# Row norms of the first layer's input from token-major squares on ScalarE, and another order of the first three column chunks

## The chip, the core and the metric

The kernel runs on one core of a Trainium2 chip. The metric is device time in microseconds (us), the median of several executions. The engines are named as the profile names them: PE (TensorE), ACT (ScalarE), DVE (VectorE), POOL (GpSimd) and SP (SyncE, which issues most of the transfers).

## What is computed

A trunk of two layers over 256 tokens of width 2048, in float32. Layer 0 is attention, layer 1 a spatial gating unit. What matters here is the start of layer 0: the RMS norm of the input, one projection, and the norms of the heads.

```python
def _rms(x, g):
    xf = x.astype(jnp.float32)
    y = xf * lax.rsqrt(jnp.mean(xf * xf, axis=-1, keepdims=True) + EPS)
    return y * g.astype(jnp.float32)

def _even_layer(x, ln_g, w_in, qk_g, sinks, w_out, rel_bias):
    h = _rms(x, ln_g).astype(x.dtype)
    z = h @ w_in
    ...
    qa, ka, va, ga, qb, kb, vb, gb = jnp.split(z, cuts, axis=-1)
    ya = _mixer_a(qa, ka, va, qk_g[0], qk_g[1], sinks, rel_bias[:, :A_HEADS])
    yb = _mixer_b(qb, kb, vb, qk_g[2], qk_g[3], rel_bias[:, A_HEADS:])
    y = jnp.concatenate([ya * jax.nn.silu(ga), yb * jax.nn.silu(gb)], axis=-1)
    return x + y.astype(x.dtype) @ w_out
```

The 16 query heads of mixer A fill two column chunks of 512, its two key and value heads together one narrow chunk of 256 columns.

## The kernel before

**Products.** A product is done one column chunk at a time (`gemm`, L100): 512 columns of weights, all 16 k tiles of 128 rows, for the two token tiles of 128. Float32 operands are split into two parts, `hi` and `lo`, and three matmuls stand for one product: `hi` by `whi` (L121), `hi` by `wlo` (L122), `lo` by `whi` (L123). A chunk has 96 matmuls, 12 for each pair of k tiles; a pair is called a tile below, numbered 0 to 7 within a chunk. Its weights come in one transfer on SP's queue (L80) into `wraw` (6 buffers); ACT casts them into `whi` (L85) and DVE subtracts to get `wlo` (L86), 4 buffers each. The two accumulators of a chunk take two of the four PSUM banks `g`; so a chunk cannot start before the chunk before the last has been copied out.

**The first chunk.** In chunk QA, the first 512 query columns of mixer A, `pre0` runs ahead of each tile. `load_hT` (L147) loads a piece of x transposed (`xT`, 256 KB), and ACT and DVE multiply it by the norm's gain and split it (`hTh` L159, `hTl` L160). The row norm itself is left out of `h`: it is applied as a scale when accumulators are copied out by ACT (`evac`, L204), so it is needed only then. `add_squares` (L171) makes it from the same transposed x: POOL squares (L175, L178) and adds up (L179) into `sqa`.

**The second chunk and the norm.** `in0` of QA is followed by the narrow k/v chunk of mixer A (`w_kva`). While it runs, `first_evac` (L113) adds up `sqa` over the partitions by eight small matmuls against `ones` (`sum_squares`, L185), DVE makes the reciprocal root (`row_rstd`, `rsqrt`), and ACT copies QA out. After that chunk come the norms of the k heads and of the q heads (`headnorm`: square on POOL L214, sums L216 and roots on DVE; `scaled`: POOL L224), then the second query chunk, QA1, the gates GA0 and GA1, and mixer B's chunks KB, QB, VB.

**The order around it.** Attention is put between matmuls by `fillers`, generators of which `gemm` advances one step twice per tile. The steps of mixer A's first half begin after the k/v chunk, wait 20 fills (`WAIT0`) and then transpose keys (`k_T`) and queries (`q_T`, L234) on PE through the single bank `t`. x itself, token major (`xr`), is wanted for the residual; its two halves of 1 MB are loaded by `load_x` (L191), written after the gates. The instructions are placed by a scheduler: each engine works in the order that it gives, and the parts of one step are spread between those of others.

Of the kernel before, what the change touches and what calls it, by code (L numbers as in the profile page):

```python
# [10 lines left out]
F32 = mybir.dt.float32  # L11
# [6 lines left out]
P = 128  # L18
S = 256
# [9 lines left out]
MAXD = 2048  # L29
L1, L2, WAIT0, WQ, WAITS = 3, 5, 20, 2, 2  # L30


@with_exitstack
def trunk(ctx, tc, x, xT, ev_g, w_in0, w_kva, qk_g, sinks, w_out0, od_g, w_in1, v_g, w_sT, b_s,
# [13 lines left out]
    def m2(shape, name):  # L48
        return mid.tile(shape, F32, tag="m2", name=name)
# [10 lines left out]
    def rsqrt(xin, n, scale):  # L60
        """(scale * xin + EPS) ** -0.5 for a [128, n] tile."""
        a = tiny.tile([P, n], F32, tag=f"ra{n}", name=nm("ra"))
        nc.vector.tensor_scalar(a, xin, scale, EPS, op0=ALU.mult, op1=ALU.add)
        y = tiny.tile([P, n], F32, tag=f"ry{n}", name=nm("ry"))
        nc.vector.tensor_scalar(y.bitcast(I32), a.bitcast(I32), -0.5, float(0x5F3759DF),
                                op0=ALU.mult, op1=ALU.add)
        t = tiny.tile([P, n], F32, tag=f"rt{n}", name=nm("rt"))
        for _ in range(3):
            nc.vector.tensor_tensor(t, y, y, op=ALU.mult)
            nc.vector.scalar_tensor_tensor(t, t, -0.5, a, op0=ALU.mult, op1=ALU.mult)  # L70
            nc.vector.scalar_tensor_tensor(y, t, 1.5, y, op0=ALU.add, op1=ALU.mult)
        return y

# [1 line left out]
    def wtile(w, kt, cw, fine=False):  # L75
# [24 lines left out]
    def gemm(aT, nkt, w, cw, pre=None, last=False):  # L100
        """act [256, 128 * nkt] @ one column chunk w (cw columns, tiled by _tiles);
        aT(kt) gives the (hi, lo) parts of act^T."""
        # (PSUM bank, token tile, first and last column)
        acc = [(psum("g", 4), 0, 0, cw), (psum("g", 4), 1, 0, cw // 2 if last else cw)]
        if last:
            acc.append((psum("g", 4), 1, cw // 2, cw))
        for k0 in range(0, nkt, 2):
            if pre is not None:
                pre(k0)
            fine = pre is not None and k0 == 0  # L110
            whi, wlo = wtile(w, k0, cw, fine)
            work = [(g, k) for g in acc for k in range(2)]
            if fine:  # L113
                work.sort(key=lambda t: t[1])
            for n, ((bank, tt, a, b), k) in enumerate(work):
                kt = k0 + k
                ah, al = aT(kt)
                sl = slice(tt * P, (tt + 1) * P)
                st, en = kt == 0, kt == nkt - 1
                o = bank[:, :b - a]  # L120
                nc.tensor.matmul(o, ah[:, sl], whi[:, k, a:b], start=st, stop=False)  # L121
                nc.tensor.matmul(o, ah[:, sl], wlo[:, k, a:b], start=False, stop=False)  # L122
                nc.tensor.matmul(o, al[:, sl], whi[:, k, a:b], start=False, stop=en)  # L123
                if n % 2:
                    fill()
        return acc if last else [g[0] for g in acc]

# [1 line left out]
    # The tensor engine's clock and the activation table are warm when the first data arrive.  # L129
    wz = cons.tile([P, P], F32, name="wz")  # L130
# [10 lines left out]

    xr = cons.tile([P, 2, D], F32, name="xr")      # residual stream, token major

# [3 lines left out]
    def load_hT(kt):  # L147
        """Normalisation gain on x^T, split; two k tiles at a time."""
        q, r = divmod(kt, 4)
# [16 lines left out]

    ones = cons.tile([P, 2], F32, name="ones")
    nc.vector.memset(ones, 1.0)
    sqa = cons.tile([P, 2, S], F32, name="sqa")

    def add_squares(kt):  # L171
        """Sum of squares of x^T over k tiles, two at a time."""
        raw = xTt[kt // 4][:, kt % 4:kt % 4 + 2, :]
        if kt == 0:
            nc.gpsimd.tensor_tensor(sqa, raw, raw, op=ALU.mult)  # L175
        else:
            sq = m2([P, 2, S], nm("sqx"))
            nc.gpsimd.tensor_tensor(sq, raw, raw, op=ALU.mult)  # L178
            nc.gpsimd.tensor_tensor(sqa, sqa, sq, op=ALU.add)  # L179

    def sum_squares():
        tp = psum("t", 1)
        for tt in range(2):
            for j in range(2):
                nc.tensor.matmul(tp[:, 2 * tt:2 * tt + 2], sqa[:, j, tt * P:(tt + 1) * P], ones,  # L185
                                 start=j == 0, stop=j == 1)
        ss0 = cons.tile([P, 2, 1], F32, name="ss0")
        nc.vector.tensor_copy(ss0, tp[:, 0:4].rearrange("p (t c) -> p t c", c=2)[:, :, 0:1])
        return ss0

# [3 lines left out]
    def row_rstd(ss, n, name):  # L194
        """ss [128, 2, m]: partial sums of squares over n columns."""
        s2 = cons.tile([P, 2], F32, name=name + "s")
        nc.vector.tensor_reduce(s2, ss, axis=AX.X, op=ALU.add)
        r = rsqrt(s2, 2, 1.0 / n)
        keep = cons.tile([P, 2], F32, name=name)
        nc.vector.tensor_copy(keep, r)  # L200
        return keep

# [1 line left out]
    def evac(acc, cw, func=AF.Copy, name="z", rs=None):  # L204
# [5 lines left out]
    def headnorm(z, nh):  # L210
        """z: [128, 2, nh*64] in place times its per-head rsqrt."""
        sq = c4([P, 2, 512], nm("sq"))
# [25 lines left out]
    def q_T(z, scale, box):  # L238
        """Queries of token tile 0 in float32, of tile 1 in two float32r parts."""
        q0 = c4([P, 4, P], nm("q0"))  # L240
# [43 lines left out]
    def bias_tile(mix, h):  # L284
        """Position bias of four heads, with the mask (and multiplicities) added."""
        bt = c4([P, 4, 256], nm("bias"))
        nc.gpsimd.dma_start(bt, bias[(mix * 16 + h) // 4].rearrange("p (h k) -> p h k", h=4))
        nc.gpsimd.tensor_tensor(bt, bt, ba[:, mix:mix + 1, :].broadcast_to([P, 4, 256]), op=ALU.add)  # L288
        return bt

    def attention(mix, h0, first_bias, qTb, kTb, vfn, ydst):
        """Eight heads h0.. of one mixer; ydst: [128, 2, 512] output (ungated)."""
        (q0, q1), (k0, kh, kl) = qTb, kTb
# [92 lines left out]
    def split_T(y, yT, q, tags):  # L386
        """y [128 tok, 2, 512] -> yT[q] = (hi, lo), each [128, 4, 256]."""
        hi, lo = c4([P, 4, S], nm("yTh"), F32R), c4([P, 4, S], nm("yTl"), F32R)
# [13 lines left out]

    QA, GA, QB, KB, VB, GB = 0, 2, 4, 6, 8, 10     # first column chunk in w_in0

# [9 lines left out]

    def pre0(k0):
        load_hT(k0)
        add_squares(k0)

    acc = in0(QA, pre0)
    box = []  # L420

    def first_evac():
        for _ in range(WAITS):
            yield
        rs = row_rstd(sum_squares(), D, "rstd0")
        box.append(rs)
        box.append(evac(acc, 512, rs=rs, name="qa"))

    fillers.append(first_evac())
    acc1 = gemm(hTk, KT, w_kva, 256)  # L430
    rs, zq = box
    qkg = cons.tile([P, 4], F32, name="qkg")
# [10 lines left out]
    dup = ka_norm(zkv)  # L443
    qk_norm(zq)
    kTa = []
# [41 lines left out]
    fillers.append(attn_a(0, zq))  # L487
    zq1 = qk_norm(evac(in0(QA + 1), 512, rs=rs, name="qa"))
    fillers.append(attn_a(1, zq1))
    gates(0, 0)  # L490
    load_x(0)
    gates(0, 1)
    load_x(1)
    for g in range(2):
# [8 lines left out]

# [1 line left out]
    g1 = cons.tile([P, KT], F32, name="g1")  # L505
# [43 lines left out]

# [1 line left out]
    rs1 = row_rstd(ss1, D, "rstd1")  # L551
# [70 lines left out]

# [1 line left out]
    for q in range(4):  # L624
# [17 lines left out]
def _tiles(w, cw):  # L642
    """[K, N] -> [N / cw, K / 256, 128, 2 * cw]: each two k tiles of a column chunk in one block."""
    k, n = w.shape
# [4 lines left out]
def _layout(x, ev_ln_g, ev_w_in, ev_qk_g, ev_sinks, ev_w_out, od_ln_g, od_w_in, od_v_g, od_w_s,  # L649
# [50 lines left out]
```

## Time and profile before

| what | value |
|---|---|
| median of 3 runs | 1183.59 us (1182.34 to 1183.89) |
| profiled execution, first to last instruction | 1182.0 us span |
| the median over that span | 1.6 us |
| busy in the span: PE, DVE, ACT, POOL | 1166.1, 661.6, 592.3, 158.8 us |
| mean DMA rate | 185 GB/s |

The profile's page gives no other time for the profiled execution than its span. The view of waits lists who waited for whom; the timeline gives each instruction by start and duration, both in us, and in brackets the idle time ahead of it and what ended that. A matmul's duration contains its way through the pipeline: matmuls of 512 columns with about 0.4 us each start about 0.23 us apart, and so the distance of starts is what a matmul costs.

### The profile page before, as it was taken

How to read it: one execution, taken by the hardware profiler on the slowest of the kernel's cores; microseconds unless marked ns; L12 is line 12 of the kernel's file. 1: busy time of each engine (PE TensorE's matmuls, PEld its weight loads, DVE VectorE, ACT ScalarE, POOL GpSimd, SP SyncE). 2: the span in 40 equal slices, each digit the busy share in tenths (PEclk: the TensorE clock that was granted, in tenths of full speed). 3: DMA queues.
4: the chain of work that ended last, by engine and by line, in shares of the span. 5: the costliest groups of instructions: out<-in, count | busy, mean ns of one | idle time of the engine just before them, and what ended most of it. 6: DMA issues, size and time to landing. Idle time of an engine off the chain costs nothing.

```text
span 1182.0 us, 14627 instructions
## 1 busy us (share of the span) xinstructions
PE 1166.1 (99%) x5554; PEld 964.1 (82%) x5554; DVE 661.6 (56%) x839; ACT 592.3 (50%) x804; POOL 158.8 (13%) x100
## 2 busy tenths in 40 slices
PE   7999999999999999999999999999999999999998
PEld 5877788788788888888888888888888888888887
DVE  8685556656645555455455655556555555544443
ACT  5447654464554454554554555454455545433332
POOL 7141201202203000021123211000000000000000
PEclk9999999999999999999999999999999999999999
DMA  7873435625526555666665545555554555566661
GB/s 252 269 255 110 143 127 180 224 91 183 207 94 213 203 180 184 201 203 213 204 199 178 210 171 189 185 188 182 177 193 162 194 194 181 184 211 201 206 212 37
DMA packets 63638, 218.37 MB, mean 185 GB/s; under 512 B 7632, under 2 KB 10320, under 8 KB 63312
## 3 DMA queue, kind: packets, MB, share of 16 engines
q1 hardware_dynamic: 60352, 209.74, 52.1%
q0 software_dynamic: 2080, 7.34, 1.9%
q8 instruction: 43, 0.70, 0.2%
q10 hardware_dynamic: 1136, 0.36, 0.1%
q14 instruction: 27, 0.22, 0.1%
HBM read 215.32 MB, written 2.10 MB: 184 GB/s over the span
## 4 chain that ended last, share of the span: by engine, by line
PE 92%; DVE 3%; DMA 1%; issue 1%; ACT 1%; POOL 1%; SPq 0%; ACTq 0%; DVEq 0%; POOLq 0%
PE g L121 28%; PE g L122 28%; PE g L123 28%; DVE wlo L86 1%; POOL wsn L587 1%; PE t L341 1%; PE s L312 1%; PE u L356 1%; DMA g<-in_od_g_dram 1%; PE u L357 1%; PE t L393 1%; PE s L315 1%; PE u L355 1%; ACT whi L85 1%; PE t L234 0%
## 5 line engine op out<-in xcount | busy, mean ns | idle before, releaser
L86 DVE TENSOR_TENSOR wlo<-wraw,whi 128x1024 fp32r<-128x1024 f32 (+1 forms) x393 | 520.8, 1329 | 425.8 <-ACT whi L85 425.4
L85 ACT CAST whi<-wraw 128x1024 fp32r<-128x1024 f32 (+1 forms) x393 | 408.4, 1041 | 494.1 <-PE g L123 474.5
L122 PE MATMUL g<-wlo,hTh 128*128 128x512 f32 (+1 forms) x1184 | 460.9, 389 | 7.0 <-DVE wlo L86 7.0
L121 PE MATMUL g<-whi,hTh 128*128 128x512 f32 (+1 forms) x1184 | 465.2, 393 | 0.0
L123 PE MATMUL g<-whi,hTl 128*128 128x512 f32 (+1 forms) x1184 | 460.1, 389 | 0.0
L122 PEld LDWEIGHTS g<-wlo,hTh 128*128 128x128 f32 x1184 | 223.0, 188 | 51.2 <-DVE wlo L86 9.6
L121 PEld LDWEIGHTS g<-whi,hTh 128*128 128x128 f32 x1184 | 222.8, 188 | 45.4 <-ACT whi L85 0.6
L123 PEld LDWEIGHTS g<-whi,hTl 128*128 128x128 f32 x1184 | 222.9, 188 | 44.6
L121 PE MATMUL g<-whi,yTh 128*128 128x512 f32 (+1 forms) x416 | 156.1, 375 | 0.0
L122 PE MATMUL g<-wlo,yTh 128*128 128x512 f32 (+1 forms) x416 | 155.3, 373 | 0.0
L123 PE MATMUL g<-whi,yTl 128*128 128x512 f32 (+1 forms) x416 | 155.2, 373 | 0.0
L121 PEld LDWEIGHTS g<-whi,yTh 128*128 128x128 f32 x416 | 78.4, 188 | 13.7
L123 PEld LDWEIGHTS g<-whi,yTl 128*128 128x128 f32 x416 | 78.3, 188 | 13.8
L122 PEld LDWEIGHTS g<-wlo,yTh 128*128 128x128 f32 x416 | 78.4, 188 | 13.6
L611 POOL TENSOR_TENSOR y<-y,gt 128x1024 f32<-128x1024 f32 x8 | 19.2, 2406 | 265.2 <-ACT gt L207 265.2
L575 POOL TENSOR_TENSOR v<-v,gv 128x1024 f32<-128x1024 f32 x8 | 21.9, 2743 | 220.1 <-ACT junk L572 220.1
L318 DVE CUSTOM_DVE_ANT_0 sb<-s,bias 128x256 f32<-128x256 f32 x32 | 13.5, 422 | 28.8 <-PE s L315 28.8
L587 POOL TENSOR_SCALAR wsn<-ws,rstdv 128x256 f32<-128x256 f32 x16 | 20.3, 1280 | 60.7 <-PE s L601 57.3
L331 ACT ACTIVATE pr<-sb,nmx 128x256 f32<-128x256 f32 x32 | 16.3, 508 | 23.0 <-DVE nmx L329 13.7
L207 ACT ACT_TABLE_LOAD x21 | 26.9, 1283 | 1.7 <-PE g L123 1.4
L288 POOL TENSOR_TENSOR bias<-bias,ba 128x1024 f32<-128x1024 f32 x8 | 20.8, 2599 | 37.7 <-DMA bias<-in_bias_dram 37.7
L593 DVE TENSOR_TENSOR vl<-v,vh 128x1024 fp32r<-128x1024 f32 x8 | 9.8, 1226 | 16.4 <-ACT vh L592 16.4
(135 smaller groups left out, 652.6 us busy)
## 6 DMA issues: line engine op xcount, KB each, us to landing
wraw<-in_w_in_dram SPq DMA_DIRECT2D x287, 512.0 KB, 4.0
wraw<-in_w_out_dram SPq DMA_DIRECT2D x96, 512.0 KB, 3.5
bias<-in_bias_dram POOLq DMA_DIRECT2D x8, 512.0 KB, 4.4
xT<-in_xT_dram SPq DMA_DIRECT2D x8, 256.0 KB, 5.1
wraw<-in_w_kva_dram SPq DMA_DIRECT2D x8, 256.0 KB, 4.2
xr<-in_x_dram SPq DMA_DIRECT2D x2, 1024.0 KB, 7.0
gv<-in_v_g_dram POOLq DMA_DIRECT2D x8, 256.0 KB, 3.0
out_dram<-o SPq DMA_DIRECT2D x7, 256.0 KB, 4.9
```

The lines of the kernel that those rows point to most:

```text
L85: nc.scalar.copy(hi[:, js, :cw], raw[:, js, :cw])
L86: nc.vector.tensor_tensor(lo[:, js, :cw], raw[:, js, :cw], hi[:, js, :cw].bitcast(F32), op=ALU.subtract)
L121: nc.tensor.matmul(o, ah[:, sl], whi[:, k, a:b], start=st, stop=False)
L122: nc.tensor.matmul(o, ah[:, sl], wlo[:, k, a:b], start=False, stop=False)
L123: nc.tensor.matmul(o, al[:, sl], whi[:, k, a:b], start=False, stop=en)
L207: nc.scalar.activation(z[:, tt, :cw], acc[tt][:, :cw], func, scale=rs[:, tt:tt + 1])
L288: nc.gpsimd.tensor_tensor(bt, bt, ba[:, mix:mix + 1, :].broadcast_to([P, 4, 256]), op=ALU.add)
L318: nc.vector.tensor_tensor_reduce(out=sb[:, 0:256], in0=sp[:, 0:256], in1=bt[:, j, :], scale=1.0, scalar=NEG, op0=ALU.add, op1=ALU.max, acc ...
L331: nc.scalar.activation(pr[:, 0:256], sb[:, 0:256], AF.Exp, bias=nmx[:, j, 1:2], accum_out=l[:, j, 1:2])
L575: nc.gpsimd.tensor_tensor(v, v, gv.unsqueeze(1).broadcast_to([P, 2, 512]), op=ALU.mult)
L587: nc.gpsimd.tensor_scalar(wsn[:, n], ws[c // 4][:, (2 * c) % 8:(2 * c) % 8 + 2, :], rsv[:, n:n + 1], None, op0=ALU.mult)
L611: nc.gpsimd.tensor_tensor(y, y, gate[0], op=ALU.mult)
```

## The change

The squares of transposed x on POOL and their sum on PE are removed. Instead each half of x in token-major form is loaded during the second chunk, and ACT squares it in four pieces with the sums of each row as a second output (`accum_out`). The second chunk is now QA1 (512 query columns), and the narrow k/v chunk the third. `X0` fills go by before the first half of x is loaded, and `XW` between a load and its Squares; with 16 fills in a chunk, the load and the Squares of the second half are written right behind chunk QA1. The later loads of x are gone, and the norm of the second q chunk follows that of k. The rest of the diff removes comments.

```diff
-L1, L2, WAIT0, WQ, WAITS = 3, 5, 20, 2, 2
+L1, L2, WAIT0, WQ, X0, XW = 3, 5, 20, 2, 4, 8
...
-    ones = cons.tile([P, 2], F32, name="ones")
-    nc.vector.memset(ones, 1.0)
-    sqa = cons.tile([P, 2, S], F32, name="sqa")
...
-            nc.gpsimd.tensor_tensor(sq, raw, raw, op=ALU.mult)
-            nc.gpsimd.tensor_tensor(sqa, sqa, sq, op=ALU.add)
...
-                nc.tensor.matmul(tp[:, 2 * tt:2 * tt + 2], sqa[:, j, tt * P:(tt + 1) * P], ones,
-                                 start=j == 0, stop=j == 1)
...
+    ss0 = cons.tile([P, 2, 4], F32, name="ss0")
+
+    def row_squares(tt, j):
+        junk = m2([P, 512], nm("junk"))
+        nc.scalar.activation(junk, xr[:, tt, j * 512:(j + 1) * 512], AF.Square,
+                             accum_out=ss0[:, tt, j:j + 1])
...
-    acc = in0(QA, pre0)
+    acc = in0(QA, load_hT)
     box = []
 
     def first_evac():
-        for _ in range(WAITS):
-            yield
-        rs = row_rstd(sum_squares(), D, "rstd0")
+        for _ in range(X0):
+            yield
+        for tt in range(2):
+            load_x(tt)
+            for _ in range(XW):
+                yield
+            for j in range(4):
+                row_squares(tt, j)
+                yield
+        rs = row_rstd(ss0, D, "rstd0")
         box.append(rs)
         box.append(evac(acc, 512, rs=rs, name="qa"))
 
     fillers.append(first_evac())
+    accq = in0(QA + 1)
+    while len(box) < 2:
+        fill()
+    rs, zq = box
+    zq1 = evac(accq, 512, rs=rs, name="qa")
+    qk_norm(zq)
     acc1 = gemm(hTk, KT, w_kva, 256)
-    rs, zq = box
...
     dup = ka_norm(zkv)
-    qk_norm(zq)
+    qk_norm(zq1)
...
     fillers.append(attn_a(0, zq))
-    zq1 = qk_norm(evac(in0(QA + 1), 512, rs=rs, name="qa"))
     fillers.append(attn_a(1, zq1))
     gates(0, 0)
-    load_x(0)
     gates(0, 1)
-    load_x(1)
```

How the instructions stand on three engines, of before and of the change (a number behind a name tells instances of a tile apart; line numbers are those of each kernel, the changed one has fewer lines):

POOL from the program's start. Before:

```order
masks.py:199 AFFINE_SELECT ident<-ident 128x128
L175 TENSOR_TENSOR sqa<-xT_104 128x512
L178 TENSOR_TENSOR sqx_137<-xT_104 128x512
L178 TENSOR_TENSOR sqx_166<-xT_160 128x512
L179 TENSOR_TENSOR sqa<-sqa,sqx_137 128x512
L179 TENSOR_TENSOR sqa<-sqa,sqx_166 128x512
L178 TENSOR_TENSOR sqx_192<-xT_160 128x512
L179 TENSOR_TENSOR sqa<-sqa,sqx_192 128x512
```

The change:

```order
masks.py:199 AFFINE_SELECT ident<-ident 128x128
L198 TENSOR_TENSOR sq_487<-qa_481 128x1024
L208 TENSOR_TENSOR qa_481<-qa_481,ry_493 128x1024
L198 TENSOR_TENSOR sq_664<-kva_661 128x2x128
L260 TENSOR_TENSOR kdup_682<-kva_661,ry_670 128x2x128 x2
```

POOL has nothing left in the first chunk; its first work is the head norm of QA, followed by that of k.

ACT from the end of the second chunk's casts to the copies of the chunks. Before (`whi_463` and `whi_481` are the last narrow casts, `whi_553` is the first of QA1, `g_100` and `g_101` hold QA):

```order
L85 CAST whi_463<-wraw_461 128x2x256
L85 CAST whi_481<-wraw_479 128x2x256
L207 ACTIVATE qa_380<-g_100,rstd_378 128x512
L207 ACTIVATE qa_380<-g_101,rstd_378 128x512
L85 CAST whi_553<-wraw_551 128x1024
L85 CAST whi_574<-wraw_572 128x1024
L85 CAST whi_592<-wraw_590 128x1024
L207 ACTIVATE kva_506<-g_323,rstd_378 128x256
L207 ACTIVATE kva_506<-g_324,rstd_378 128x256
```

The change (`whi_434` is QA1's last cast, `whi_510` the first narrow one, `g_98` and `g_99` hold QA, `g_299` and `g_300` QA1):

```order
L85 CAST whi_434<-wraw_432 128x1024
L172 ACTIVATE junk_455,ss_97<-xr 128x512
L172 ACTIVATE junk_457,ss_97<-xr 128x512
L172 ACTIVATE junk_459,ss_97<-xr 128x512
L172 ACTIVATE junk_461,ss_97<-xr 128x512
L85 CAST whi_510<-wraw_508 128x2x256
L85 CAST whi_528<-wraw_526 128x2x256
L191 ACTIVATE qa_481<-g_98,rstd_479 128x512
L191 ACTIVATE qa_481<-g_99,rstd_479 128x512
L85 CAST whi_546<-wraw_544 128x2x256
L191 ACTIVATE qa_484<-g_299,rstd_479 128x512
L191 ACTIVATE qa_484<-g_300,rstd_479 128x512
```

Four Squares stand between QA1's casts and the narrow ones, and both query chunks are copied out among the narrow casts.

DVE around the transposed keys of mixer A (`kl`). Before (`rt_709` and `ry_707` belong to the norm of QA1's heads):

```order
L71 SCALAR_TENSOR_TENSOR ry_707<-rt_709,ry_707 128x16
L69 TENSOR_TENSOR rt_709<-ry_707 128x16
L86 TENSOR_TENSOR wlo_863<-wraw_860,whi_862 128x1024
L70 SCALAR_TENSOR_TENSOR rt_709<-rt_709,ra_705 128x16
L71 SCALAR_TENSOR_TENSOR ry_707<-rt_709,ry_707 128x16
L263 TENSOR_TENSOR kl_772<-t_773,kh_771 128x512
L86 TENSOR_TENSOR wlo_905<-wraw_902,whi_904 128x1024
L247 SCALAR_TENSOR_TENSOR q_788<-t_789,gain,q_788 128x256
```

The change:

```order
L86 TENSOR_TENSOR wlo_936<-wraw_933,whi_935 128x1024
L86 TENSOR_TENSOR wlo_963<-wraw_960,whi_962 128x1024
L86 TENSOR_TENSOR wlo_999<-wraw_996,whi_998 128x1024
L247 TENSOR_TENSOR kl_908<-t_909,kh_907 128x512
L86 TENSOR_TENSOR wlo_1041<-wraw_1038,whi_1040 128x1024
L231 SCALAR_TENSOR_TENSOR q_924<-t_925,gain,q_924 128x256
```

The head norm of QA1 has left this place; it stands a chunk earlier. From the second tile of chunk VB on, the rows of every engine are the same in both but for line numbers.

## Rows read from the trace of the kernel before

**Rows 1.** The page's busy time, us (share of the span) and instructions of each engine.

```profile
PE 1166.1 (99%) x5554; PEld 964.1 (82%) x5554; DVE 661.6 (56%) x839; ACT 592.3 (50%) x804; POOL 158.8 (13%) x100
```

**Rows 2.** Waits of PE, whole span: us in total, times, longest.

```profile
PE g L122 <- DVE wlo L86: 7.0, 5, 2.0
```

**Rows 3.** Timeline of PE: start, duration, instruction, [idle before and what ended it].

```profile
5.18 0.73 PE L121 MATMUL g<-whi,hTh 128*128 128x512 f32 x2
...
10.60 0.50 PE L122 MATMUL g<-wlo,hTh 128*128 128x512 f32 x1 [1.17 <-DVE wlo L86]
...
21.13 0.62 PE L122 MATMUL g<-wlo,hTh 128*128 128x512 f32 x1
...
24.53 0.41 PE L121 MATMUL g<-whi,hTh 128*128 128x512 f32 x1
...
30.06 0.40 PE L123 MATMUL g<-whi,hTl 128*128 128x512 f32 x1
...
37.82 0.28 PE L121 MATMUL g<-whi,hTh 128*128 128x256 f32 x1
...
39.97 0.95 PE L185 MATMUL t<-ones,sqa 128*128 128x2 f32 x8
40.78 0.36 PE L121 MATMUL g<-whi,hTh 128*128 128x256 f32 x1
...
83.08 0.63 PE L234 MATMUL t<-ident,qa 128*128 128x128 f32 x4 [0.68 <-ACT k L264]
...
86.01 0.66 PE L234 MATMUL t<-ident,qa 128*128 128x128 f32 x4 [0.68 <-ACT q L250]
```

**Rows 4.** Windows: us, PE, PEld, DVE, ACT, POOL busy, PEclk, DMA share, GB/s.

```profile
17.80:24.60 6.80, 4.94 (x15) 3.52 (x14) 6.80 (x5) 3.24 (x6) 6.61 (x5) 0.75 0.60 221
24.60:28.60 4.00, 3.35 (x14) 2.17 (x12) 4.00 (x4) 1.67 (x2) 3.91 (x3) 1.00 0.21 66
...
37.80:50.00 12.20, 12.20 (x104) 12.18 (x103) 7.92 (x21) 7.23 (x11) 0.00 (x0) 1.00 0.92 283
```

**Rows 5.** Groups of DVE instructions, 8 to 28.6 us: busy us, mean ns | idle.

```profile
L160 DVE SCALAR_TENSOR_TENSOR hTl<-xT,g,hTh 128x256 fp32r<-128x256 f32 x9 | 11.5, 1312 | 0.0
L86 DVE TENSOR_TENSOR wlo<-wraw,whi 128x1024 fp32r<-128x1024 f32 x5 | 10.6, 2116 | 0.5 <-ACT whi L85 0.5
```

**Rows 6.** Timeline of DVE and POOL.

```profile
8.68 1.87 DVE L86 TENSOR_TENSOR wlo<-wraw,whi 128x1024 fp32r<-128x1024 f32 x1 [0.47 <-ACT whi L85]
...
29.60 0.87 DVE L160 SCALAR_TENSOR_TENSOR hTl<-xT,g,hTh 128x256 fp32r<-128x256 f32 x2
30.39 1.21 DVE L86 TENSOR_TENSOR wlo<-wraw,whi 128x1024 fp32r<-128x1024 f32 x1
...
82.45 2.61 DVE L86 TENSOR_TENSOR wlo<-wraw,whi 128x1024 fp32r<-128x1024 f32 x1
...
82.08 1.90 POOL L224 TENSOR_TENSOR qa<-qa,ry 128x1024 f32<-128x1024 f32 x1 [6.68 <-DVE ry L71]
```

**Rows 7.** Timeline of ACT: casts of tiles 3, 4 and 6 of chunk QA.

```profile
13.01 1.05 ACT L85 CAST whi<-wraw 128x1024 fp32r<-128x1024 f32 x1 [0.81 <-DMA wraw<-in_w_in_dram]
...
15.28 1.05 ACT L85 CAST whi<-wraw 128x1024 fp32r<-128x1024 f32 x1 [0.42 <-DMA wraw<-in_w_in_dram]
...
19.30 1.04 ACT L85 CAST whi<-wraw 128x1024 fp32r<-128x1024 f32 x1 [0.22 <-DMA wraw<-in_w_in_dram]
```

**Rows 8.** Groups by shape, whole span: layer 0's Squares of the residual on ACT.

```profile
L522 ACT ACTIVATE junk<-xr 128x512 f32<-128x512 f32 x8 | 4.9, 619 | 0.0
...
L522 ACT ACTIVATION_READ_ACCUMULATOR junk<-xr 128x1 f32 x8 | 1.5, 186 | 0.0
```

**Rows 9.** The two loads of x, line L192, from issue to landing.

```profile
DMA to landing us min/median/max: 5.0/7.0/9.0
```

**Rows 10.** Timeline of DVE: first and last instruction of the row norm.

```profile
40.96 0.16 DVE L188 COPY ss<-t 128x2 f32<-128x2 f32 x1 [0.16 <-PE t L185]
...
44.89 0.17 DVE L200 COPY rstd<-ry 128x2 f32<-128x2 f32 x1
```

More of the change, by code (lines that the diff above doesn't have):

```diff
@@ L165, in hTk @@
         return hi[:, kt % 4, :], lo[:, kt % 4, :]
-    ones = cons.tile([P, 2], F32, name="ones")
-    nc.vector.memset(ones, 1.0)
-    sqa = cons.tile([P, 2, S], F32, name="sqa")
[L171 to L177, printed above, removed]
-            nc.gpsimd.tensor_tensor(sq, raw, raw, op=ALU.mult)
-            nc.gpsimd.tensor_tensor(sqa, sqa, sq, op=ALU.add)
[L181 to L184, printed above, removed]
-                nc.tensor.matmul(tp[:, 2 * tt:2 * tt + 2], sqa[:, j, tt * P:(tt + 1) * P], ones,
-                                 start=j == 0, stop=j == 1)
-        ss0 = cons.tile([P, 2, 1], F32, name="ss0")
-        nc.vector.tensor_copy(ss0, tp[:, 0:4].rearrange("p (t c) -> p t c", c=2)[:, :, 0:1])
-        return ss0
+    ss0 = cons.tile([P, 2, 4], F32, name="ss0")
[3 more added lines that the diff above has]
+                             accum_out=ss0[:, tt, j:j + 1])
     def load_x(tt):
@@ L413, in trunk @@
     in0 = lambda c, pre=None: gemm(hTk, KT, w_in0[c], 512, pre)
-    def pre0(k0):
-        load_hT(k0)
-        add_squares(k0)
-    acc = in0(QA, pre0)
+    acc = in0(QA, load_hT)
     box = []
     def first_evac():
-        for _ in range(WAITS):
+        for _ in range(X0):
             yield
-        rs = row_rstd(sum_squares(), D, "rstd0")
+        for tt in range(2):
[6 more added lines that the diff above has]
+        rs = row_rstd(ss0, D, "rstd0")
         box.append(rs)
```

## The prediction

> **What bounds the kernel now.** The list of engines comes first: TensorE (PE) is busy 1166.1 of the 1182.0 us span [rows 1]. So time can come out only where PE idles, where it runs matmuls slowly, or where it does work that can be dropped. The waits of PE, longest first, then say where it idles: its largest entry is PE on `wlo` of L86, 7.0 us in five waits [rows 2]. The timeline of PE puts these waits into the first column chunk. That chunk (QA, 96 matmuls of 512 columns) begins at 5.18, and the next chunk's first matmul, of 256 columns, starts at 37.82 [rows 3]: 32.6 us. From the start 30.06 to that one lie 34 matmuls in a row without a wait [rows 3], 0.228 us each, and 96 of them would take 21.9 us. The first chunk is thus 10.7 us longer than its matmuls; from 37.8 to 50 PE is busy 12.20 of 12.20 us [rows 4], and over the whole span 99%.
>
> Why is `wlo` late? The groups of VectorE (DVE) instructions between 8 and 28.6 us show `wlo` at 2116 ns and `hTl` at 1312 ns each [rows 5]. The timeline of DVE right behind that stretch shows the same shapes at 1.21 us for one `wlo` and 0.87 us for two `hTl` [rows 6]. A k-tile pair needs one `wlo` and two `hTl`: 4.74 us of DVE in the slow stretch, 2.08 us behind it, against 12 x 0.228 = 2.74 us of PE. So DVE paces the chunk while it is slow, and PE would pace it otherwise.
>
> What makes DVE slow is read from the windows [rows 4]. From 24.6 to 28.6 GpSimd (POOL) is busy 3.91 of 4.00 us and the DMA share is only 0.21, and DVE still runs slowly. From 37.8 to 50 the DMA share is 0.92, POOL does nothing, and PE is never idle. The slowness goes with POOL, not with DMA traffic. All of POOL's work there is the squares of L175, L178 and L179, which end at 28.6.
>
> **The change part by part.** *The squares leave POOL* (15 instructions: L175 once, L178 and L179 seven times each). The loads and the casts on ScalarE (ACT) keep their order in chunk QA, and ACT's casts wait there for loads, so I take their times over: the cast of tile 3 starts at 13.01, of tile 4 at 15.28, of tile 6 at 19.30 [rows 7], each 1.05 us, with the fast `wlo` (1.21) behind it. Tile 1 gets its `wlo` 0.66 us earlier than the 10.60 at which PE took it [rows 3], since that one took 1.87 instead of 1.21 [rows 6]: at 9.94. Ten matmuls remain: PE ends tile 1 at 12.2. Tile 2 costs 2.74 and ends at 15.0. Tile 3's `wlo` is ready at 13.01 + 1.05 + 1.21 + 0.05 = 15.3; one matmul needs only `whi` and covers to 15.2, a stall of 0.1, so tile 3 ends at 17.9. Tile 4's `wlo` is ready at 17.6, tile 6's at 21.6 while PE gets to it at 23.3; from here PE paces. Tiles 4 to 7 take 4 x 2.74 = 11.0, and chunk QA ends at 28.8 instead of 37.8: **-9.0 us**.
>
> *The eight sums over partitions on PE* (L185, float32 against `ones`) go. They start at 39.97 and the next narrow matmul at 40.78, 0.81 us later; the 18 narrow matmuls from 37.82 to 39.97 start 0.12 apart [rows 3]: **-0.7 us**.
>
> *ACT gets eight Squares instead*, 619 ns and a 186 ns accumulator read each [rows 8], 6.4 us in all. Their cover is ACT's waiting: with four `whi` buffers ACT waits for PE once per tile, and has 1.05 us of casting in 2.74. The first four stand behind the cast of chunk QA1's third tile (with six raw buffers its load of `x` gets out at about 18, behind the `wlo` of chunk QA's tile 4; a load of half of `x` lands 5.0 to 9.0 after issue [rows 9]; ACT reaches the Squares near 27). The other four are the tight place, since before them nothing of the row norms can be finished. The cast of QA1's last tile waits for PE to finish that chunk's fourth tile, 28.8 + 11.0 = 39.8; the cast ends at 40.8, four Squares at 44.0. The row-norm chain on DVE with two narrow `wlo` in between took from 40.96 to 45.06 in the trace [rows 10], 4.1 us: 48.1. The first half of QA's accumulators, 128x512 like a Square, is then copied out, which I put at 0.7 us by the Square's 619 ns: 48.8. That frees the bank that the third chunk's first matmul needs, and PE gets there at 28.8 + 21.9 = 50.7. Margin 1.9 us: costs nothing.
>
> *The two loads of x* move up on SP's queue: the first from between the narrow loads to ahead of QA1's fourth tile, the second from ahead of GA's fourth tile to ahead of the narrow loads. Each is 1 MB, as long on the wire as two tiles, and SP runs six raw buffers and four split ones ahead of PE: nothing for both.
>
> *The order of the chunks* (QA, QA1, narrow k/v instead of QA, k/v, QA1) leaves PE's matmuls the same in number. Mixer A's attention begins 20 fillers after the k/v chunk in both, so it now lies over GA1 rather than GA, and the norm of the second q chunk is done before it. That touches two waits of PE: the transposes of `qa` at 83.08 and 86.01 waited 0.68 each [rows 3]. The first came behind `kl`, queued on DVE after the norm of `zq1`; the second behind a `wlo` that took 2.61 us while POOL's L224 scaled `zq1` [rows 6]. Neither neighbour is there now. I walk both places with 1.05 for a cast, 1.21 for a `wlo`, and a cast that starts when PE frees its buffer, and about 0.1 and 0.2 us are left: **-1.1 us**. Its bounds are +1.5 (two new waits like them, over KB's norm) and -1.4.
>
> The sum: -9.0 - 0.7 - 1.1 = -10.8. The profiled execution spans 1182.0, so 1171.2; the runs' median, 1183.59, is 1.6 above that span, which I add back: **1172.8 us**. From the second tile of chunk VB on the instructions of every engine stand as before, so nothing should give this back later.
>
> **The rivals.**
> *The clock falls all the same (chance 0.15).* In the trace the granted clock averages 0.75 from 17.8 to 24.6 [rows 4]: between 21.13 and 24.53 eight matmuls start 0.425 us apart [rows 3], the lower of the two levels (1.2 against 2.4 GHz), after PE had idled part of every tile since 8.5 us. There the loss hid in the wait for `wlo`. Should the clock fall as long again, with PE as the bound, the 8 x (0.425 - 0.228) = 1.6 us are paid: 1174.4. Against it: ahead of that point one wait of half a us is left (1.17 less 0.66, in tile 1 [rows 3]) and some of 0.1, where most of the 7.0 us of waits [rows 2] had fallen. The Trainium skill (TensorE: Matmul & The Clock Gate, "HAM oscillation — how this bites in real kernels") says that idle gaps between groups of matmuls put PE back to half clock. By that rule, if the gap in tile 1 counts, the time is the 1174.4 of this rival; the trace agrees so far as its one fall came after repeated gaps, and no run here shows what a single one does.
>
> *The narrow chunk runs dry (0.24).* A narrow tile lasts PE only 12 x 0.12 = 1.44 us, and the whole norm of the first q chunk (a square and a scaling on POOL, twelve instructions on DVE) now runs under it, with both copies out of QA1 on ACT ahead of the fourth narrow cast. I find about 1 us of slack per tile. A `wlo` that meets the scaling loses 2.61 - 1.21 = 1.4 us [rows 6]; two such meetings, or one and a late bank, give 1.5 to 3 us: 1174.3 to 1175.8.
>
> *DVE does not get faster (0.03).* If the loads slowed DVE, chunk QA stays at 32.6 us, and 1.8 us are left: 1181.8, within 0.2%. Against it stand the two windows above.
>
> *Slower: the second half of x is late (0.03).* ACT works in order, and behind its wait for that half stand the narrow casts and the copy that frees the bank. It must land by 40.8 + 1.9 = 42.7 to cost nothing; each us after that is a us for PE. All that is won is gone at 53.5, and over 2.4 us are lost past 55.9: 1186 and up. The load is issued near 26, behind the split of QA1's second tile, and would have to take 27 us where the two in the trace took 5.0 and 9.0 [rows 9].
>
> **How the numbers follow.** My forecast has 0.55. The range reaches up over the clock case and the whole narrow case with 1 us for spread between runs: 1176.8. Down it takes the last 0.3 of the two waits, half a us in tile 1, and 1.5 us for the spread with waits around them that I leave as they are: 1170.5. About 2 in 10 lie outside. A measurement tells 0.2% (2.4 us) from no change; 1181.2 is that bound, and forecast, clock and narrow case all lie under it: faster 0.94, same 0.03, slower 0.03.
>
> **What would show it.** Right: chunk QA's last matmul starts near 28.6; `wlo` takes 1.2 us and two `hTl` 0.9 from 8 to 28 us; POOL is empty till about 48; PE's waits for `wlo` sum to under 2 us. PE goes from QA1 into the narrow chunk without a gap near 50.7. The transposes of `kdup` and `qa` wait under 0.3 us. Wrong: a `wlo` still near 2 us with POOL empty; a PE gap at the start of the narrow chunk with ACT's Squares or the load of x as releaser; a granted clock under 1 near 20 us; waits of PE for `wlo` inside the narrow chunk.

## The result and the profile after

| | median of the runs | over the kernel before | span of the profiled execution |
|---|---|---|---|
| before | 1183.74 us | | 1182.0 us |
| changed | 1171.53 us (1171.01 to 1172.93) | 0.9897 (95% interval 0.9883 to 0.9912) | 1169.2 us |

The change saves 12.2 us by the medians and 12.8 us in the spans of the two profiled executions. Forecast were 10.8 us and 1172.8 us, with a range of 1170.5 to 1176.8 that holds the result. A second set of runs of the changed kernel, told below, gave 0.9899 (0.9884 to 0.9913).

The page of the changed kernel, busy times: PE is busy 4.1 us less than before, 99% of a span that is 12.8 us shorter.

```profile
PE 1162.0 (99%) x5546; PEld 963.0 (82%) x5546; DVE 647.5 (55%) x837; ACT 595.2 (51%) x818; POOL 135.7 (12%) x85
```

PE's waits in the whole span of the changed kernel (total, times, longest, in us). The 7.0 us on `wlo` of [rows 2] are down to a single wait of 0.5:

```profile
PE t L218 <- ACT k L248: 1.0, 1, 1.0
PE t L136 <- DVE wz L131: 1.0, 1, 1.0
PE g L121 <- ACT whi L85: 0.6, 1, 0.6
PE g L122 <- DVE wlo L86: 0.5, 1, 0.5
```

DVE's groups between 8 and 28.6 us of the changed kernel stand against [rows 5]: `wlo` fell from 2116 to 1225 ns, `hTl` from 1312 to 478.

```profile
L86 DVE TENSOR_TENSOR wlo<-wraw,whi 128x1024 fp32r<-128x1024 f32 x10 | 12.2, 1225 | 3.9 <-ACT whi L85 3.6
L160 DVE SCALAR_TENSOR_TENSOR hTl<-xT,g,hTh 128x256 fp32r<-128x256 f32 x13 | 5.7, 478 | 0.0
```

A window of the changed kernel, columns as in [rows 4]. In the stretch where the clock had averaged 0.75 it is 1.00, PE is busy throughout, and POOL is empty. The DMA share is 1.00 there, against 0.60 before: transfers follow PE faster, and DVE is fast under a full DMA load.

```profile
17.80:24.60 6.80, 6.80 (x31) 5.63 (x31) 6.20 (x10) 5.78 (x9) 0.00 (x0) 1.00 1.00 398
```

The timeline of PE in the changed kernel answers to [rows 3]. The narrow chunk, now the third, begins at 50.95 with no wait in brackets, behind the 192 matmuls of two full chunks. The 97th of them, the first of QA1, starts at 29.19, which is where chunk QA ended. The chunk behind the narrow one starts at 62.47. The last row is the first transpose of mixer B (`zb`), which in the kernel before started at 222.13.

```profile
5.63 0.71 PE L121 MATMUL g<-whi,hTh 128*128 128x512 f32 x2
...
9.23 0.73 PE L121 MATMUL g<-whi,hTh 128*128 128x512 f32 x2 [0.60 <-ACT whi L85]
10.49 0.50 PE L122 MATMUL g<-wlo,hTh 128*128 128x512 f32 x1 [0.53 <-DVE wlo L86]
...
29.19 0.39 PE L121 MATMUL g<-whi,hTh 128*128 128x512 f32 x1
...
50.73 0.39 PE L123 MATMUL g<-whi,hTl 128*128 128x512 f32 x1
50.95 0.28 PE L121 MATMUL g<-whi,hTh 128*128 128x256 f32 x1
...
62.47 0.40 PE L121 MATMUL g<-whi,hTh 128*128 128x512 f32 x1
...
209.72 0.60 PE L218 MATMUL t<-ident,zb 128*128 128x128 f32 x4
```

So the 12.8 us of the spans divide like this:

| part | before | after | won |
|---|---|---|---|
| end of chunk QA | 37.82 | 29.19 | 8.6 |
| narrow chunk, first matmul to the next chunk's first | 12.40 (37.82 to 50.22) | 11.52 | 0.9 |
| everything else up to the first `zb` transpose | 171.91 | 169.01 | 2.9 |
| from there to the end | 959.9 | 959.5 | 0.4 |

The third part is what is left of 222.13 - 209.72 = 12.41 after the first two.

### The profile page after: what moved, and what is told of

Same layout as the page of the kernel before. It is cut to its first block, busy times and chain, and to the rows that moved or that the text cites. A ratio compares the mean times of both kernels' runs of the same rounds, so it can differ in the third digit from the quotient of the medians.

```text
span 1169.2 us, 14610 instructions
## 1 busy us (share of the span) xinstructions
PE 1162.0 (99%) x5546; PEld 963.0 (82%) x5546; DVE 647.5 (55%) x837; ACT 595.2 (51%) x818; POOL 135.7 (12%) x85
## 4 chain that ended last, share of the span: by engine, by line
PE 96%; DVE 1%; POOL 1%; ACT 1%; DMA 0%; issue 0%; SPq 0%; ACTq 0%; POOLq 0%
PE g L121 30%; PE g L123 29%; PE g L122 29%; PE t L325 1%; POOL wsn L577 1%; PE s L296 1%; PE t L377 1%; PE s L299 1%; PE u L340 1%; PE u L341 1%; PE t L218 1%; PE u L339 1%; DVE wlo L86 0%; DMA wraw<-in_w_in_dram 0%; ACT whi L85 0%
## 5 line engine op out<-in xcount | busy, mean ns | idle before, releaser
L86 DVE TENSOR_TENSOR wlo<-wraw,whi 128x1024 fp32r<-128x1024 f32 (+1 forms) x393 | 514.0, 1312 | 427.3 <-ACT whi L85 426.5
L583 DVE TENSOR_TENSOR vl<-v,vh 128x1024 fp32r<-128x1024 f32 x8 | 9.8, 1225 | 16.4 <-ACT vh L582 16.4
```

The lines of the kernel that those rows point to most:

```text
L86: nc.vector.tensor_tensor(lo[:, js, :cw], raw[:, js, :cw], hi[:, js, :cw].bitcast(F32), op=ALU.subtract)
```

## The experiments

Unless said otherwise an edit is made to the changed kernel. Two theories stand behind the first four: that POOL's squares slowed DVE by being on POOL at the same time, and the rival that DVE was slow for another reason (loads, the order of chunks), so that the gain came from the order or from DMA.

**e1: the kernel before, without the squares on POOL.** The old order and the eight sums on PE stay.

```diff
+    nc.vector.memset(sqa, 8.0)
...
-        add_squares(k0)
```

> The kernel before with one part left out: POOL's fifteen squares and sums of chunk QA; their sum tile is filled with a constant once, so the row norms of layer 0 are not those of the input. The order of the chunks and the eight small matmuls stay. My theory (POOL's squares slow DVE, and DVE paces PE): a wlo takes 1.2 us from 8 to 28 us, chunk QA goes from 32.6 to about 23.5 us, the three waits of PE that stood at 83, 86 and 101 stay (now near 74, 77 and 92, 2.3 us together), and the time is 1183.6 - 9 = about 1174.5. Rival 1 (the loads slow DVE or the chunk): chunk QA stays at 32 us and the time near 1183. Rival 2 (the gain hangs on the order of the chunks): a gain of under 3 us.

Measured: 1174.56 us, 0.9924 (0.9906 to 0.9943), that is 9.0 us less than before by the ratio and 9.6 by the medians. DVE in e1, 8 to 28.6 us (wide forms apart):

```profile
L86 DVE TENSOR_TENSOR wlo<-wraw,whi 128x1024 fp32r<-128x1024 f32 x7 | 8.6, 1223 | 1.0 <-ACT whi L85 1.0
L160 DVE SCALAR_TENSOR_TENSOR hTl<-xT,g,hTh 128x256 fp32r<-128x256 f32 x14 | 6.2, 480 | 0.0
```

PE in e1, the first matmul of QA and of the narrow chunk:

```profile
7.10 0.71 PE L121 MATMUL g<-whi,hTh 128*128 128x512 f32 x2
...
30.59 0.28 PE L121 MATMUL g<-whi,hTh 128*128 128x256 f32 x1
```

Chunk QA lasts 23.5 us instead of 32.6, with the old order of chunks. Since `sqa` is ready at once, the scheduler put the eight sums at the program's start, where they push QA's first matmul to 7.10 (5.63 in the changed kernel: 1.5 us). The narrow chunk without them takes 11.5 us to the next chunk's first matmul. The two waits at the transposes of `qa` stayed, 0.64 and 0.67 us.

**e2: the squares put back on POOL, their result unused.** The order and the Squares on ACT are those of the change.

```diff
-    acc = in0(QA, load_hT)
+    sqa = cons.tile([P, 2, S], F32, name="sqa")
+    def pre0(kt):
+        load_hT(kt)
+        raw = xTt[kt // 4][:, kt % 4:kt % 4 + 2, :]
+        if kt == 0:
+            nc.gpsimd.tensor_tensor(sqa, raw, raw, op=ALU.mult)
+        else:
+            sq = m2([P, 2, S], nm("sqx"))
+            nc.gpsimd.tensor_tensor(sq, raw, raw, op=ALU.mult)
+            nc.gpsimd.tensor_tensor(sqa, sqa, sq, op=ALU.add)
+    acc = in0(QA, pre0)
```

> The changed kernel with POOL's fifteen squares and sums put back into chunk QA, where nothing reads them. My theory: wlo is back at about 2.1 us, chunk QA back at about 32 us, the granted clock falls near 20 us as it did before, the waits between 60 and 130 us stay away, and the time is 1171.5 + 9 = about 1180.5. Rival 1 (the loads): no change, 1171.5. Rival 2 (order alone): no change either.

Measured: 1180.86 us, 0.9979 (0.9965 to 0.9993); 9.3 us of the change's gain are gone. Chunk QA lasts 32.8 us (5.75 to 38.54), and PE has no wait from 60 to 200 us. DVE's groups in e2, 8 to 28.6 us, have the durations of the kernel before:

```profile
L160 DVE SCALAR_TENSOR_TENSOR hTl<-xT,g,hTh 128x256 fp32r<-128x256 f32 x10 | 12.7, 1305 | 0.0
L86 DVE TENSOR_TENSOR wlo<-wraw,whi 128x1024 fp32r<-128x1024 f32 x5 | 10.6, 2118 | 0.1
```

The window of e2 beside them: POOL full, DVE never idle, the clock down again.

```profile
17.80:24.60 6.80, 5.99 (x20) 4.15 (x19) 6.80 (x5) 4.48 (x7) 6.57 (x6) 0.82 0.90 337
```

e1 and e2 together show it from both sides: take the POOL squares away and chunk QA is short, put them back and it is long, whatever the order.

How POOL slows DVE can be read from single rows. These are one `wlo` and two POOL instructions of the kernel before, in chunk QA:

```profile
13.35 2.05 DVE L86 TENSOR_TENSOR wlo<-wraw,whi 128x1024 fp32r<-128x1024 f32 x1
...
13.11 1.22 POOL L178 TENSOR_TENSOR sqx<-xT 128x512 f32<-128x512 f32 x1
14.40 2.17 POOL L179 TENSOR_TENSOR sqa<-sqa,sqx 128x512 f32<-128x512 f32 x1
```

The square ends at 14.33 and `wlo` 1.07 us later, at 15.40; the add, begun at 14.40, ends 1.17 us after `wlo`, at 16.57. Alone, `wlo` takes 1.21 and a square 1.04. So in these rows each of the two engines does nearly its whole work after the other's instruction has ended. The changed kernel has the same in its narrow chunk, where a `wlo` of 128x512, 0.69 us alone, meets the square of the q heads:

```profile
49.17 1.98 DVE L86 TENSOR_TENSOR wlo<-wraw,whi 128x512 fp32r<-128x512 f32 x1 [1.84 <-ACT whi L85]
...
48.72 1.89 POOL L198 TENSOR_TENSOR sq<-qa 128x1024 f32<-128x1024 f32 x1 [47.43 <-ACT qa L191]
```

POOL ends at 50.61, `wlo` 0.54 later.

**e3: the kernel before with the new order of chunks alone**, and a second profile of it, **e3b**. Squares on POOL and sums on PE stay.

```diff
+    accq = in0(QA + 1)
+    while len(box) < 2:
+        fill()
     rs, zq = box
+    zq1 = evac(accq, 512, rs=rs, name="qa")
+    qk_norm(zq)
     acc1 = gemm(hTk, KT, w_kva, 256)
-    rs, zq = box
...
-    qk_norm(zq)
+    qk_norm(zq1)
...
-    zq1 = qk_norm(evac(in0(QA + 1), 512, rs=rs, name="qa"))
```

> The kernel before with the new order of the chunks alone: QA, QA1, k/v, squares still on POOL and summed on PE. My theory: chunk QA still takes about 32.6 us; the waits of PE at 83, 86 and 101 us (2.3 us) do not come back behind the new order, so the time falls by 2.3 to 2.9 us, to about 1181. If the missing 1 to 2 us of my forecast came from somewhere else than the order, the gain is 1 us or less. Rival (order alone is the gain): 1172.

Measured: 1183.01 us, 0.9989 (0.9979 to 0.9998): 1.2 us less, between 0.2 and 2.5. Chunk QA still takes 32.4 us (5.75 to 38.16), so the order alone does not shorten it. The expectation was too large. It had counted all three waits that the trace of before has between 60 and 200 us, and one of these comes and goes, as the next three profiles show.

**b1, b2: the kernel before, two more profiles.**

> The kernel before, unchanged, profiled a second time, to see which of its waits in the middle are fixed. Theory 1 (the two waits at the transposes of qa belong to the old order, the one of 0.93 us at 101.03 was an accident of that execution): waits of 0.6 to 0.7 near 83 and 86 stand again, none near 101. Rival (all three are fixed, and so the order is worth 2.3 us in every run): all three stand again. First narrow matmul at 37.8 within 0.5 in both cases.

> The same once more: with three profiles of the kernel before, a wait that stands in one of three is an accident, one that stands in all three belongs to the order. Theory 1: the sum of TensorE's waits from 60 to 200 us is 1.3, not 2.3.

> The order of the chunks alone, profiled a second time. Its first profile showed no wait from 60 to 200 us, and its time was 1.7 us under the median of its runs. Theory 1 (the order takes the waits of qa's transposes away for good): none there again, under 0.3 us in sum from 60 to 200. Rival (such waits come and go with the execution, in this order too): one or two of 0.6 us or more, and a time near 1183.

Measured, one execution each: b1 1183.10 us, b2 1182.60, e3b 1182.31. PE's waits between 60 and 200 us in b1:

```profile
PE t L234 <- ACT k L264: 0.7, 1, 0.7
PE t L234 <- ACT q L250: 0.7, 1, 0.7
PE t L341 <- ACT pt L343: 0.6, 1, 0.6
```

In the profile first shown the third entry was 0.9 us, in b1 0.6 (where none was expected), and in b2 it is absent; e1, with the old order, does not have it either. The two at the transposes of `qa` stand in all three profiles of before with 0.7 each, and e3b, like e3 and like both profiles of the changed kernel, has no wait of PE from 60 to 200 us. So the order takes away those two waits, 1.4 us, and the third comes and goes. From 200 to 400 us e3b had 2.2 us of waits on the same bank `t`, where e3 had 1.0: those vary too.

**a1: the changed kernel again**, beside e5 and e6 on one chip.

> The changed kernel once more, beside the three below on one chip. A ratio to the kernel before near 0.9897; chunk QA about 23.4 us, the third chunk without a wait ahead of it, no wait of PE of over 0.3 us between 60 and 130 us.

Measured: 1171.49 us, 0.9899 (0.9884 to 0.9913), span 1169.6. Chunk QA takes 23.8 us (5.76 to 29.59), the narrow chunk begins without a wait, and there is none from 60 to 200 us.

**e4: POOL busy with writes only.** Sixty fills of a buffer that nothing reads.

```diff
+    pw = cons.tile([P, 2, S], F32, name="pw")
+    for _ in range(60):
+        nc.gpsimd.memset(pw, 1.0)
```

> The changed kernel with sixty fills of a 128x512 tile on POOL during chunk QA: POOL is busy there, but only writes. If what slows DVE is POOL's reading from SBUF while DVE reads two inputs from it, wlo stays at 1.2 us, chunk QA ends as in the changed kernel and the time stays near 1171.5. If any work of POOL slows DVE, wlo goes to about 2 us while the fills run, and up to 9 us are lost.

Measured: 1171.96 us, one execution. DVE's `wlo` in e4, 8 to 28.6 us:

```profile
L86 DVE TENSOR_TENSOR wlo<-wraw,whi 128x1024 fp32r<-128x1024 f32 x9 | 11.0, 1225 | 5.8 <-ACT whi L85 5.7
```

The window of e4 (POOL's busy time is the fifth):

```profile
8.00:28.60 20.60, 19.67 (x84) 15.19 (x83) 15.38 (x21) 14.32 (x22) 18.53 (x37) 1.00 0.96 363
```

POOL is busy 18.53 of 20.60 us, `wlo` stays at 1225 ns, and chunk QA ends at 29.41. A POOL that is busy writing does not slow DVE.

**e7: POOL reading one operand**, 32 multiplications by a constant beside chunk QA, their result unused.

```diff
+    pr1 = cons.tile([P, 2, S], F32, name="pr1")
+    def pre1(kt):
+        load_hT(kt)
+        raw = xTt[kt // 4][:, kt % 4:kt % 4 + 2, :]
+        for _ in range(4):
+            nc.gpsimd.tensor_scalar(pr1, raw, 1.0, None, op0=ALU.mult)
-    acc = in0(QA, load_hT)
+    acc = in0(QA, pre1)
```

> The changed kernel with 32 POOL instructions in chunk QA that read a 128x512 piece of x transposed once and write one tile, in place of the squares that read two inputs. If any read of SBUF by POOL holds DVE up, wlo takes near 2 us while they run and chunk QA takes over 28 us. If two inputs on POOL are needed, wlo stays at 1.2 us and chunk QA at 23.4 us.

Measured: 1184.23 us, one execution, and this time says nothing on the question. One such instruction takes POOL about 1.7 us, so the 32 ran until 61.7 us, the square of the q heads on POOL came late, DVE, which works in order, waited 12.79 us for it, and PE waited behind DVE. The durations in chunk QA do answer. DVE's groups in e7, 8 to 28.6 us:

```profile
L86 DVE TENSOR_TENSOR wlo<-wraw,whi 128x1024 fp32r<-128x1024 f32 x10 | 13.5, 1375 | 1.4 <-ACT whi L85 1.4
L160 DVE SCALAR_TENSOR_TENSOR hTl<-xT,g,hTh 128x256 fp32r<-128x256 f32 x13 | 7.9, 639 | 0.0
```

Neither expectation came: `wlo` takes 12% more than alone, `hTl` 34%; with the two-operand squares and adds of e2 it is 73% and 173%. Nor does DVE wait here for whole POOL instructions: between 8 and 23 us the rows of a single `wlo` show 1.21 to 1.52 us beside POOL instructions of 1.73. Chunk QA still ends in time, the narrow chunk's first matmul being at 50.94. The Trainium skill (SBUF — State Buffer, "Who interferes with whom") says that a DVE instruction with two SBUF inputs contends with a GpSimd instruction that reads SBUF and not with one that only writes it. e4 agrees for writes (1225 against 1225 ns) and e2 for reads (2118). That one-operand reads cost so much less than two-operand ones is in e7 alone. POOL also reads more slowly there, one operand of 128x512 in 1.73 us where the squares and adds of e2 read two in 1.38 and 1.71, so e7 does not part the number of operands from the rate of reading.

**e5: the second half of x squared three times**, to find the margin of the tight place, ACT's Squares ahead of the copies of QA.

```diff
-                row_squares(tt, j)
+                for _ in range(3 if tt else 1):
+                    row_squares(tt, j)
```

> The changed kernel with the four Squares of the second half of x done three times each (the sums are the same), all ahead of the copy that frees chunk QA's bank. My theory of the tight place: in the changed kernel the copy's first half is done near 48.0 and PE comes to the narrow chunk at 50.95, a margin of 2.9 us. Eight Squares more take 8 x 0.62 = 5.0 us and two narrow casts that now stand ahead of the copy 1.2 us, so the narrow chunk begins 3 to 4 us late, and the time is 3 to 4 us longer than the changed kernel's. Rival (ACT's work is hidden here whatever it is): no change.

Measured: 1177.76 us, 0.9954 (0.9939 to 0.997): 6.3 us over a1. PE in e5:

```profile
50.65 0.39 PE L123 MATMUL g<-whi,hTl 128*128 128x512 f32 x1
54.72 0.58 PE L121 MATMUL g<-whi,hTh 128*128 128x256 f32 x1 [3.68 <-ACT qa L191]
55.09 0.41 PE L122 MATMUL g<-wlo,hTh 128*128 128x256 f32 x1
55.31 0.41 PE L123 MATMUL g<-whi,hTl 128*128 128x256 f32 x1
```

The window of e5 that holds the narrow chunk, with a granted clock of 0.84:

```profile
50.00:72.00 22.00, 18.32 (x116) 17.25 (x115) 14.01 (x38) 11.56 (x20) 5.06 (x3) 0.84 0.61 193
```

The wait came where and as long as expected, 3.68 us, released by the copy of QA's bank. ACT began that copy at 53.98, when the row norms were there:

```profile
53.98 2.42 ACT L191 ACTIVATE qa<-g,rstd 128x512 f32<-128x512 f32 x4 [2.29 <-DVE rstd L184]
```

What was not expected is the rest. After that one wait the narrow matmuls start 0.21 us apart instead of 0.12 until 60.2, at a granted clock of 0.50 from 54 to 60 (the lower level), and the narrow chunk takes 13.95 us to its last matmul instead of 11.39. 3.7 and 2.6 make the 6.3 of the medians; the two profiled spans differ by 5.7, since e5's chunk QA1 ended 0.5 earlier than that of a1.

**e6: mixer A's attention 12 fills earlier.**

```diff
-L1, L2, WAIT0, WQ, X0, XW = 3, 5, 20, 2, 4, 8
+L1, L2, WAIT0, WQ, X0, XW = 3, 5, 8, 2, 4, 8
```

> The changed kernel with 8 fills instead of 20 ahead of mixer A's first transposes, which puts kl on DVE one wlo behind the head norm of QA1, and POOL's scaling of QA1 beside the next wlo, as in the kernel before. My theory (those neighbours made the two waits): the transposes of qa wait about 0.6 us each again, and the time grows by about 1.2 us. Rival (the waits belong to the place over GA, or to chance): no waits there and no change.

Measured: 1178.44 us, 0.9959 (0.9945 to 0.9973): 7.0 us over a1, where 1.2 were expected. The direction is as expected, the size is not, and only the first of the two transposes of `qa` waited. PE in e6:

```profile
77.09 0.39 PE L123 MATMUL g<-whi,hTl 128*128 128x512 f32 x1
81.86 1.12 PE L218 MATMUL t<-ident,qa 128*128 128x128 f32 x4 [4.38 <-ACT k L248]
...
83.63 0.63 PE L123 MATMUL g<-whi,hTl 128*128 128x512 f32 x1
84.06 0.63 PE L121 MATMUL g<-whi,hTh 128*128 128x512 f32 x1
```

The bank `t` of the key transposes at 74.83 was freed only at 81.8. DVE in e6 shows why:

```profile
75.85 2.35 DVE L70 SCALAR_TENSOR_TENSOR rt<-rt,ra 128x16 f32<-128x16 f32 x1
...
80.72 0.69 DVE L247 TENSOR_TENSOR kl<-t,kh 128x512 fp32r<-128x512 f32 x1
```

`kl`, the low part of the keys, is taken from `t`, and ACT's last copy out of that bank, for which PE waited, followed it at 81.44. `kl` stood on DVE behind the whole norm of the second q chunk, which 20 fills would have let go by; and one instruction of that norm, 0.17 us elsewhere, took 2.35, that is 2.2 us more, beside POOL's add of the bias, which has two operands and ended at 78.17:

```profile
75.77 2.40 POOL L272 TENSOR_TENSOR bias<-bias,ba 128x1024 f32<-128x1024 f32 x1 [3.19 <-DMA bias<-in_bias_dram]
```

Again the clock fell behind the wait: 0.86 from 80 to 92 us, with matmuls 0.43 apart at 83.63. From 81.86 on, the transposes and the four matmuls behind them took 2.62 us, the next such group, which starts at 86.24, only 1.36. PE's waits add up to 8.2 us over the span of e6, against 3.2 in a1; these 5.0 and the 1.3 of the clock are 6.3 of the 6.6 us between the two spans (1176.2 and 1169.6). So the first of the two waits of before is borne out as one for `kl` behind the norm. That POOL's scaling of QA1 made the second one is not shown: the transposes at 86.24 did not wait. With the new order too, 8 fills are too few.

## Why the prediction was right

Its likeliest case came, and the steps one by one:

*What paces chunk QA: right.* DVE was slow because of POOL's squares, not of the loads. `wlo` was put at 1.21 us and two `hTl` at 0.87; they took 1.225, and 0.87 to 0.88 in the rows of pairs. e1 and e2 show the cause by removal and by putting back. e4 shows that it is not POOL's being busy, for writes alone cost nothing; e7 shows that reading one operand costs little, and does not say whether the number of operands or the rate of reading makes the difference.

*-9.0 for chunk QA: right, 8.6 in the spans.* From its first matmul the chunk was to take 28.8 - 5.18 = 23.6 us, and took 29.19 - 5.63 = 23.6. It ended 0.4 late because the first matmul came 0.45 later (e3 and both further profiles of before start anywhere from 5.1 to 5.8, so that is spread). The wait for `wlo` in tile 1, worked out as 1.17 - 0.66 = 0.51, is the 0.53 at 10.49. The 0.60 ahead of it, for a cast that waited for its weights, was not in the walk; tile 1 was to take 7.0 us from the chunk's start and took 7.2, and the stall of 0.1 in tile 3 did not come, so small errors cancel here.

*-0.7 for the eight sums: right, a little small.* The narrow chunk is 0.9 us shorter, at 11.5 us, and as long in e1, where the sums stand elsewhere.

*The Squares on ACT cost nothing: right, with more margin than worked out.* This is the timeline of ACT in the changed kernel at the tight place:

```profile
40.27 1.06 ACT L85 CAST whi<-wraw 128x1024 fp32r<-128x1024 f32 x1 [1.66 <-PE g L123]
41.23 0.62 ACT L172 ACTIVATE junk<-xr 128x512 f32<-128x512 f32 x1
...
43.09 0.61 ACT L172 ACTIVATE junk<-xr 128x512 f32<-128x512 f32 x1
...
47.37 1.27 ACT L191 ACTIVATE qa<-g,rstd 128x512 f32<-128x512 f32 x2 [1.03 <-DVE rstd L184]
```

The cast, forecast to end at 40.8, began at 40.27; the Squares stand 0.62 apart, since the accumulator reads of 0.19 lie beside the next Square, so four take 2.5 us and not 3.2. The chain of the row norms ended at 47.3, 3.5 us after it began, where 4.1 were taken over from before. The first copy is out near 48.0 (half of the 1.27 from 47.37), where 48.8 was forecast, and PE needs the bank at 50.95: a margin of 2.9 us instead of 1.9. e5 tests that margin: its first copy starts at 53.98, 6.6 us after the 47.37 here, and 6.6 less 2.9 is 3.7, the 3.68 that PE waited.

*The order of the chunks, -1.1: the term that was too small.* The forecast left about 0.3 of the two waits at the transposes of `qa`, and left everything else around them as it was. Both waits went altogether, 1.4 us, in two profiles of the change and two of the order alone; by the runs' times the order gives 1.2 (0.2 to 2.5). The profile it was reckoned from also had the 0.9 us at 101.03, which is missing in other executions of the same kernel: that part of the span's gain is luck. And a wait costs PE more than its bracket. These are rows of the kernel before; the transposes that follow the first two stand at 83.08 and 86.01 in [rows 3]:

```profile
82.01 0.39 PE L121 MATMUL g<-whi,hTh 128*128 128x512 f32 x1
...
84.94 0.40 PE L122 MATMUL g<-wlo,hTh 128*128 128x512 f32 x1
...
99.71 0.39 PE L122 MATMUL g<-wlo,hTh 128*128 128x512 f32 x1
101.03 0.55 PE L341 MATMUL t<-ident,pr 128*128 128x128 f32 x3 [0.93 <-ACT pt L343]
```

From matmul to transpose it is 1.07, 1.07 and 1.32 us. Where nothing waits, the same steps take 0.23 and 0.27 in the changed kernel (93.33 to 93.56, 96.31 to 96.58) and 0.34 in b2 (99.56 to 99.90). The bracket counts from the end of the matmul ahead, 0.39 after its start, and so leaves out what overlap would have hidden. The three waits thus cost 2.6 us, of the 2.9 in the third row of the table.

In the spans the change won 2.0 us more than forecast: 0.4 less in chunk QA, 0.2 more from the sums, 1.8 more in the middle, and 0.4 behind the first `zb` transpose, which is not assigned. The median of the changed kernel's runs lies 2.3 us over its profiled span, where the forecast added 1.6; that takes 0.7 back, and the forecast lay 1.3 us above the measured median.

*The rivals.* The clock did not fall: 1.00 where it had averaged 0.75, with waits of 0.60 and 0.53 ahead. Where it did fall, the price was higher than the rival's 1.6 us: in e5 one wait of 3.7 us cost 2.6 us more, and there no wait for DVE hides it. The Trainium skill (TensorE: Matmul & The Clock Gate, "HAM oscillation — how this bites in real kernels") has idle gaps between groups of matmuls put PE back to half clock; e5 and e6 agree for gaps of 3.68 and 4.38 us, and after the gaps of up to 1.0 us in the changed kernel no fall shows. The narrow chunk did not run dry: no wait stands between 50.95 and 62.47. The meetings that this rival feared did come, the `wlo` of 1.98 us shown above and one of 1.56 beside POOL's scaling, and the chunk's slack held them. The second half of x was not late (for the first, ACT waited 1.22 us at 28.95, and no wait of PE came of it), and the slow DVE did not stay.

No version faster than the changed kernel was found. The waits that PE has left in it add up to 3.4 us in five places, one of which, that on `wz`, lies ahead of all matmuls of the chunks.

## What to carry to other kernels

When an engine's instructions of one shape take much longer in one stretch than in the next, compare the two stretches engine by engine before blaming transfers: here DVE ran at under half its pace as long as POOL read two operands, and it ran at full pace under a DMA share of 1.00. Moving work to an engine that has to wait anyway is free only while the instruction that the bound engine needs next still comes in time, so work out that margin first and test it by doing the moved work twice or three times. Count waits that come and go in single executions apart from those that stand in every profile: two more profiles of the kernel before would have told 0.9 us of luck from 1.4 us of order.

## What was not expected of the hardware

- POOL's writes alone left DVE's durations as they were (1225 ns with POOL 90% busy); POOL with one operand read lengthened `wlo` to 1375 ns, with two operands to 2118.
- A tiny DVE instruction of 128x16, 0.17 us elsewhere, took 2.35 us beside a two-operand POOL instruction of 2.40 us (e6). In five rows of three sizes DVE's instruction ended 0.03, 0.54, 0.54, 1.08 and 1.08 us after POOL's, each 0.13 to 0.15 less than it takes alone (0.17, 0.69, 0.69, 1.21 and 1.22): what is added goes by how much of the other engine's instruction is left, not by DVE's own size. The rows are those at 75.85 and 87.11 in e6, 49.17 and 57.56 in the changed kernel, and 82.45 in [rows 6]. `kl` at 80.72 in e6, with one operand in PSUM, took its usual 0.69 us while a POOL instruction ran from 79.81 to 82.56.
- One single wait of 3.7 us was followed by matmuls at a granted clock of 0.50 for 5.5 us, a loss of 2.6 us (e5); three waits of 0.5 to 1.0 us in the changed kernel (0.60, 0.53 and the one of 1.04 at the `zb` transposes) by none.
- An ACT Square with its row sums costs 0.62 us in a row of them, the 0.19 us of the accumulator read being hidden. In e5, where three in turn write the same sums, two of three take 0.75 to the next one.
